# One hybrid encoder layer on one core: reciprocal square roots from eleven VectorE instructions to one GpSimd power, and an order chosen out of 24 drawn plans

## The chip, the core and the metric

The kernel runs on one core of a Trainium2 chip. The metric is the device time of one launch in microseconds (us); lower is better. The kernel before takes 2738.26 us (median of three runs, 2738.12 to 2742.08).

## What is computed

One layer of a bidirectional encoder on a sequence of 2048 tokens of width 1024, all in float32. A normed input is projected once, and the columns go to three groups of heads: attention in a window of 128, a state-space model that runs forward and backward in chunks of 128, and cross attention to 256 memory tokens. The three outputs are joined, projected and added to the input, and a squared-ReLU MLP follows.

```python
h = rmsnorm(x, norm_mix_w[i])
q, k, v, z, xbc, dt_raw, qx = jnp.split(h @ w_in[i], split_idx, axis=-1)
q = partial_rope(rmsnorm(q, q_norm_w[i]), pos)      # per head; k likewise
attn_out = windowed_gqa(q, k, v, attn_sink[i])
ssd_out = bidirectional_ssd(z, xbc, dt_raw, ...)    # ends in rmsnorm per group
xatt_out = memory_cross_attention(qx, mem, ...)     # rmsnorm of q, k and mem
x = x + jnp.concatenate([attn_out, ssd_out, xatt_out], axis=-1) @ w_out[i]
x = x + jnp.square(jax.nn.relu(rmsnorm(x, norm_mlp_w[i]) @ w_mlp_up[i])) @ w_mlp_down[i]
```

Every `rmsnorm` needs the reciprocal square root of a mean of squares: one number per token, or per token and head.

## The kernel before, in words

Matrix products in float32 precision are made of three faster ones: each operand is split into a high part (a cast on ScalarE) and a low part (a subtraction on VectorE or GpSimd), and high·high, high·low and low·high are added in PSUM. Most of TensorE's instructions are such products of a 128x128 stationary tile with 512 moving columns.

The program has three stages. **Stage 1** (`stage1`, L1113) goes over the sequence in two halves, the second half first. For each half it splits x, makes keys, values and time steps (`kv_products`, `kvdt_tiles`), sums the squares of the rows of x (`x_square`, `x_stats`), makes twelve columns of the convolved state-space input (`xbc_col`), and then queries for the memory and the window two token tiles at a time (`xattn_pair`, `q_pair`). In between run the memory's keys and the backward states. **Stage 2** goes over 16 token tiles with window attention and the forward state-space scan. **Stage 3** is the output projection of pairs of token tiles (`out_pair`), the norm before the MLP (`mid`), and the MLP (`seven` products in place of eight per 2x2 block).

The reciprocal square root is the function `rsqrt` (L497). It works on a small tile of 128 partitions by n numbers, where n is 2 to 16, and issues eleven VectorE instructions: two `tensor_scalar` (a first guess from the bits of the number, and minus half the number), and three Newton steps of three instructions. Each reads what the one before wrote. It is called 40 times: 24 times in stage 1 (keys 4, memory 2, rows of x 2, memory queries 8, window queries 8) and 16 times in stage 3 (8 in `out_pair`, 8 in `mid`). In `head_norm` (L666) the result is multiplied by the row's factor on VectorE, then by the whole tile on GpSimd; `rope` (L691) rotates the first 16 columns of each head with four GpSimd instructions per tile, and only then TensorE transposes the tile.

No engine's order is written by hand. Each call such as `nc.vector.tensor_tensor` is recorded as an operation with a cost and its dependencies (`Program.add`, L201; costs in `cost`, L176). `plan` (L287) then plays the program through with these costs: of the operations of an engine that are ready it takes the one that stands first in the program among those that are "safe", which means that a margin has passed since their last input was ready. `margin` (L275) sets that margin by the kinds of the two operations: 3000 ns where a DMA waits, 5000 ns before a product that fills half the array, 1500 ns after a DMA, 400 ns where TensorE waits for another engine, 800 ns otherwise. The plan also hands out the eight PSUM banks, and never lets GpSimd and a VectorE instruction on SBUF run at once. `schedule` issues all operations in that order, so in the profile they all bear the line L414.

Names in the views: `small` holds the small tiles of the norms, `const` and `late` hold tables; X, W, A, B, C, E and Z are regions of SBUF that are used anew in each stage; `bank` is PSUM.

Of the kernel before, what the change touches and what calls it, by code (L numbers as in the profile page):

```python
# [10 lines left out]
F32 = mybir.dt.float32  # L11
F32R = mybir.dt.float32r
I32 = mybir.dt.int32
AF = mybir.ActivationFunctionType
ALU = mybir.AluOpType
# [4 lines left out]
P = 128  # L20
# [15 lines left out]
NCOL, NROW = sum(n for _, n in COLS), sum(n for _, n in ROWS)  # L36
# [37 lines left out]
class Program:  # L74
# [101 lines left out]
    def cost(self, eng, name, args, kw, aps):  # L176

        n = max(self.free(args[0] if args else kw["out"]), 1)
        isap = lambda x: isinstance(x, (View, bass.AP))
        if eng == "PE":  # L180
            if name == "transpose":
                return 109
            return 108 if n < 32 else n / 2.4 + 13 if args[1].dtype == F32R and n >= 256 else n * 4 / 2.4 + 6
        if eng == "ACT":
            n_ap = sum(isap(kw.get(k)) for k in ("bias", "scale", "accum_out"))
            return 93 * n_ap + 0.834 * n + (50 if isinstance(args[1], View) and args[1].psum else 93)
        if eng == "DVE":
            if name == "reciprocal":
                return 69 + 6.25 * n
            n = max([n] + [self.free(a) for a in aps])  # L190
            if name == "memset":
                return 9 + 1.04 * n
            ap_scalar = any(isap(x) and self.free(x) == 1 for x in args[2:4]) and "scalar" in name
            fast = name in ("tensor_copy", "tensor_scalar") and not any(isinstance(a, View) and a.psum for a in aps)
            return 69 + (0.52 if fast else 1.041) * n + (61 if ap_scalar else 0)
        if eng == "POOL":
            bcast = any(d[0] == 0 and d[1] > 1 for a in aps[1:] for d in a.ap.ap[1:])
            return 148 + (1.667 if bcast else 2.1) * n if name == "tensor_tensor" else 40 + 1.6 * n
        return 475

# [70 lines left out]
            self.vuse[v] += 1  # L271
        ops.append(o)

    @staticmethod
    def margin(o, q):  # L275

        if q.eng == "SP":
            return 3000
        if q.eng == "PE" and q.half:
            return 5000  # L280
        if o.eng == "SP":
            return 1500
        if q.eng == "PE" and o.eng != "PE":
            return 400
        return 0 if o.eng == q.eng or o.eng == "PE" else 800

    def plan(self):  # L287

        engs = ["", "PE", "ACT", "POOL", "DVE", "SP"]
        free = dict.fromkeys(engs, 0.0)  # L290
# [5 lines left out]
        bank, vend = {}, {}  # L296
# [3 lines left out]
        order = []  # L300
# [5 lines left out]
        while len(order) < len(ops):  # L306
            best = None
            for e in engs:
                t = free[e]
# [14 lines left out]
            o = ops[i]  # L324
            if e == "PE" and pe_half and i != pe_last + 1 and pe_last + 1 in re:
# [4 lines left out]
                o = ops[i]  # L330
            elif e == "PE" and pe_mode and not o.half:
                same = [q for q in re if ops[q].half]
                if same:
# [4 lines left out]
                    o = ops[i]  # L338
# [9 lines left out]
            if o.new:  # L348
                got = [heapq.heappop(banks) for _ in o.new]
# [8 lines left out]
            d = o.dur  # L358
            if e == "PE":
                if o.half and pe_half == (o.dur, not o.half[1]):  # L360
                    d, pe_half = 20, None
# [32 lines left out]
                if q.ndep == 0:  # L394
                    heapq.heappush(future[q.eng], (q.ready, q.idx))
        order.sort()
        self.span, self.order, self.bank = max(free.values()), order, bank

    def schedule(self):
        self.plan()  # L400
# [60 lines left out]
class Hybrid:  # L461
# [34 lines left out]

    def rsqrt(self, pool, v, n):  # L497

        nc = self.nc
        y = pool.tile([P, 32], F32, "nr_y")[:, :n]  # L500
        h = pool.tile([P, 32], F32, "nr_h")[:, :n]
        t = pool.tile([P, 32], F32, "nr_t")[:, :n]
        nc.vector.tensor_scalar(y.bitcast(I32), v.bitcast(I32), -0.5, 1597463007.0, ALU.mult, ALU.add)
        nc.vector.tensor_scalar(h, v, -0.5, None, ALU.mult)
        for _ in range(3):
            nc.vector.tensor_tensor(t, y, y, ALU.mult)
            nc.vector.tensor_tensor(t, t, h, ALU.mult)
            nc.vector.scalar_tensor_tensor(y, t, 1.5, y, ALU.add, ALU.mult)
        return y

    def ps(self):
# [2 lines left out]

    def constants(self):
        nc, a = self.nc, self.a
        sizes = dict(ident=128, ones=128, eps=1, cols=NCOL, r1=16)
        self.mem.use("const", F32, **{"c_" + k: (n, 1) for k, n in sizes.items()})
        sizes = dict(triU=128, triL=128, amask=768, rows=NROW, dt=512, acs=512, wst=512, dec=512, edge=48, negA=32, nsk=8)
        self.mem.use("late", F32, **{"c_" + k: (n, 1) for k, n in sizes.items()})  # L520

        def c(name, shape):
            return self.mem.tile([P] + shape, F32, "c_" + name)

        self.eps = c("eps", [1])
        nc.vector.memset(self.eps, EPS)
        nc.scalar.activation(self.eps, self.eps, AF.Copy)
        self.ident = c("ident", [P])
        make_identity(nc, self.ident)
        self.ones = c("ones", [P])  # L530
        nc.gpsimd.memset(self.ones, 1.0)
        self.triU = c("triU", [P])
        self.triL = c("triL", [P])
        for t, sgn in ((self.triU, 1), (self.triL, -1)):
            nc.gpsimd.affine_select(out=t, in_=self.ones, compare_op=ALU.is_ge, fill=0.0, base=0,
                                    pattern=[[sgn, P]], channel_multiplier=-sgn)
        self.mask = c("amask", [6 * P])
        nc.gpsimd.memset(self.mask, 0.0)
        for o, sgn in ((0, 1), (2, -1), (3, 1), (5, 1)):
            m = self.mask[:, o * P:(o + 1) * P]  # L540
            nc.gpsimd.affine_select(out=m, in_=m, compare_op=ALU.is_ge, fill=NEG, base=0,
                                    pattern=[[sgn, P]], channel_multiplier=-sgn)

        cols, rows = c("cols", [NCOL]), c("rows", [NROW])
        first = NCOL - 256
        self.load(cols[:, :first], a["cols"][:, :first])

        def cut(t, table, name, shape=None):
            at = sum(n for k, n in table[:[k for k, _ in table].index(name)])
            v = t[:, at:at + dict(table)[name]]  # L550
            return v.rearrange("p (a b) -> p a b", a=shape[0]) if shape else v

        self.w_mix, self.w_mem, self.w_mlp, self.w_ssd, self.cb, self.sd = (
            cut(cols, COLS, n) for n in ("w_mix", "w_mem", "w_mlp", "w_ssd", "cb", "sd"))
        self.cw, self.cos, self.sin = cut(cols, COLS, "cw", (NXC,)), cut(cols, COLS, "cos", (NJ,)), cut(cols, COLS, "sin", (NJ,))
        for v in (cut(cols, COLS, "cw"), self.cb):
            nc.vector.tensor_scalar(v, v, 0.5, None, ALU.mult)
        self.qw, self.kw, self.xqw, self.xkw, self.sink, self.dtb, self.al = (
            cut(rows, ROWS, n) for n in ("qw", "kw", "xqw", "xkw", "sink", "dtb", "al"))
        self.r1 = c("r1", [NJ])  # L560
        self.dt = c("dt", [NJ, 32])
        self.acs = c("acs", [NJ, 32])
        self.wst = c("wst", [NJ, 32])
        self.dec = c("dec", [NJ, 32])
        self.edge = c("edge", [NXC, 4])
        self.negA = c("negA", [32])
        self.nsk = c("nsk", [8])
        yield
        self.load(cols[:, first:], a["cols"][:, first:])
        self.load(rows, a["rows"].rearrange("(o n) -> o n", o=1).broadcast_to([P, NROW]))  # L570
        nc.vector.tensor_scalar(self.qw, self.qw, 0.125, None, ALU.mult)
        nc.vector.tensor_tensor(self.xkw, self.xkw, self.xqw, ALU.mult)
        nc.scalar.activation(self.negA, self.al, AF.Exp)
        nc.vector.tensor_scalar(self.negA, self.negA, -1.0, None, ALU.mult)
        nc.vector.tensor_scalar(self.nsk, self.sink, -1.0, None, ALU.mult)
        yield

    def memory(self):
        m = self.mem
        m.use("small", F32, nr_y=(32, 3), nr_h=(32, 3), nr_t=(32, 3), nr_v=(32, 3), xmx=(32, 2), xsm=(32, 2),  # L580
              amx=(32, 3), ang=(32, 3), asm=(32, 3), aes=(32, 3), rm=(32, 1), s2=(32, 2))

    def memory1(self):
# [1181 lines left out]
```

## Time and profile before

| | us |
|---|---|
| runs: median (lowest, highest) | 2738.26 (2738.12, 2742.08) |
| profiled execution: span, first to last instruction | 2734.9 |
| what lies around the span, median less span | 3.4 |
| TensorE products busy | 2706.3 (99%) |
| VectorE busy | 1900.8 (70%) |
| ScalarE busy | 1331.6 (49%) |
| GpSimd busy | 554.2 (20%) |

A busy TensorE is not TensorE at its peak, since the ends of its instructions are modelled; but where it is not busy it waits. In a row of waits, "PE bank <- POOL B" reads: TensorE, about to write PSUM, was released last by a GpSimd instruction that wrote region B. In a timeline a row gives start, length, engine, output and inputs, the count of merged instructions, and in brackets the idle time ahead of it and who ended it.

### The profile page before, as it was taken

Reading aid. Unit: us, or ns where it says so; the run is one execution under the profiler, and the core shown is the slowest. Engines: PE = TensorE matmul, PEld = TensorE weight load, DVE = VectorE, ACT = ScalarE, POOL = GpSimd, SP = SyncE. Lnnn points to the kernel's source line nnn. Section 1 sums busy time; section 2 is a strip of 40 time slices with the busy share of each in tenths; the row PEclk is TensorE's granted clock in tenths of the full one; section 3 lists DMA queues with packets and bytes.
Section 4 is the critical chain, followed back from the end, with each engine's and each line's share of the span. In section 5 each row is a group of like instructions: output and inputs, shape, how many; then the busy total and the mean of one; then the engine's idle time right before and its main releaser. Section 6 shows DMA issues by size and latency. Waiting matters only on the chain.

```text
span 2734.9 us, 37074 instructions
## 1 busy us (share of the span) xinstructions
PE 2706.3 (99%) x13486; PEld 2236.3 (82%) x13486; DVE 1900.8 (70%) x3102; ACT 1331.6 (49%) x2229; POOL 554.2 (20%) x488
## 2 busy tenths in 40 slices
PE   8999999999999999999999999999999999999999
PEld 7788887787778888788888888888888888888887
DVE  6884689956677686776666785857757584857666
ACT  6545534353567676733333543535353443535352
POOL 3203444455445554410101000000000000000000
PEclk9999999999999999999999999999999999999999
DMA  6651446545877786865555954536272745435241
GB/s 239 213 182 59 133 147 190 172 158 177 268 251 235 214 257 205 271 204 200 193 192 202 342 195 146 170 102 214 80 259 93 253 162 169 154 119 197 90 165 62
DMA packets 264886, 501.40 MB, mean 183 GB/s; under 512 B 26096, under 2 KB 99072, under 8 KB 264704
## 3 DMA queue, kind: packets, MB, share of 16 engines
q1 hardware_dynamic: 264704, 499.04, 55.3%
q8 instruction: 106, 1.74, 0.3%
q14 instruction: 76, 0.62, 0.1%
HBM read 381.51 MB, written 117.45 MB: 182 GB/s over the span
## 4 chain that ended last, share of the span: by engine, by line
PE 92%; DVE 2%; POOL 2%; ACT 1%; issue 1%; DMA 1%; SPq 0%; DVEq 0%; ACTq 0%; POOLq 0%
PE bank L414 92%; POOL B L414 1%; DVE B L414 1%; DVE A L414 1%; POOL E L414 1%; DVE small L414 0%; DMA Z<-in_w_out_dram 0%; ACT C L414 0%; SPq L414 0%; DMA W<-erow_d 0%; DVE W L414 0%; ACT A L414 0%; ACT B L414 0%; POOL W L414 0%; DVE X L414 0%
## 5 line engine op out<-in xcount | busy, mean ns | idle before, releaser
L414 PE MATMUL bank<-X,late 128*128 128x512 f32 x1792 | 552.3, 389 | 0.0
L414 PE MATMUL bank<-A,E 128*128 128x512 f32 (+2 forms) x1152 | 404.8, 380 | 1.1 <-ACT A L414 0.7
L414 PE MATMUL bank<-X,A 128*128 128x512 f32 (+1 forms) x1264 | 396.1, 390 | 0.2 <-DMA A<-v_d 0.2
L414 PEld LDWEIGHTS bank<-X,late 128*128 128x128 f32 x1792 | 336.3, 188 | 69.6
L414 PE MATMUL bank<-late,C 128*128 128x512 f32 x896 | 348.6, 389 | 0.0
L414 PE MATMUL bank<-late,E 128*128 128x512 f32 x896 | 348.6, 389 | 0.0
L414 PE MATMUL bank<-W,X 128*128 128x512 f32 (+1 forms) x1536 | 339.4, 373 | 6.5 <-ACT W L414 5.8
L414 PE MATMUL bank<-X,W 128*128 128x512 f32 x1344 | 324.3, 398 | 0.7 <-ACT E L414 0.6
L414 PE MATMUL bank<-X,X 128*128 128x512 f32 x1216 | 317.6, 401 | 0.6 <-DVE X L414 0.6
L414 PEld LDWEIGHTS bank<-W,X 128*128 128x128 f32 x1536 | 265.8, 190 | 51.5 <-ACT W L414 5.8
L414 PEld LDWEIGHTS bank<-X,W 128*128 128x128 f32 x1344 | 250.8, 189 | 55.8 <-issue 3.4
L414 PEld LDWEIGHTS bank<-X,X 128*128 128x128 f32 x1216 | 225.2, 188 | 56.0 <-issue 8.9
L414 PEld LDWEIGHTS bank<-A,E 128*128 128x128 f32 x1152 | 211.7, 188 | 43.0 <-issue 2.8
L414 PEld LDWEIGHTS bank<-X,A 128*128 128x128 f32 (+1 forms) x1264 | 192.5, 173 | 50.5 <-issue 3.5
L414 DVE TENSOR_TENSOR A<-Z,late 128x1024 fp32r<-128x1024 f32 x100 | 121.9, 1221 | 149.0 <-ACT late L414 142.6
L414 DVE TENSOR_TENSOR B<-B,bank 128x512 f32<-128x512 f32 x286 | 189.7, 680 | 33.3 <-PE bank L414 32.6
L414 PEld LDWEIGHTS bank<-late,E 128*128 128x128 f32 x896 | 168.2, 188 | 34.9
L414 PEld LDWEIGHTS bank<-late,C 128*128 128x128 f32 x896 | 168.2, 188 | 34.8
L414 ACT CAST late<-Z 128x1024 fp32r<-128x1024 f32 x100 | 105.1, 1051 | 140.0 <-PE bank L414 101.3
L414 ACT ACTIVATE C<-C,small 128x384 f32<-128x384 f32 (+1 forms) x256 | 143.8, 598 | 36.0 <-DVE small L414 35.9
L414 ACT ACTIVATE W<-W 128x512 f32<-128x512 f32 x224 | 134.4, 627 | 48.9 <-DVE W L414 45.9
L414 DVE SCALAR_TENSOR_TENSOR B<-B,const 128x1022 f32<-128x1022 f32 (+1 forms) x96 | 146.0, 1524 | 3.9 <-ACT B L414 3.0
(178 smaller groups left out, 4259.3 us busy)
## 6 DMA issues: line engine op xcount, KB each, us to landing
X<-xc_d SPq DMA_DIRECT2D x112, 1024.0 KB
xc_d<-E SPq DMA_DIRECT2D x56, 512.0 KB
Z<-in_w_z_dram SPq DMA_DIRECT2D x32, 512.0 KB
W<-erow_d SPq DMA_DIRECT2D x64, 256.0 KB
X<-in_w_up_dram SPq DMA_DIRECT2D x32, 512.0 KB
A<-in_w_up_dram SPq DMA_DIRECT2D x32, 512.0 KB
X<-in_w_down_dram SPq DMA_DIRECT2D x32, 512.0 KB
A<-in_w_down_dram SPq DMA_DIRECT2D x32, 512.0 KB
```

Source lines behind the costliest of these rows:

```text
L414: o.fn(*[fix(x) for x in o.args], **{k: fix(x) for k, x in o.kw.items()})
```

## The change

First, `rsqrt` becomes one GpSimd instruction, `tensor_tensor` with the operation power, whose second operand is a constant tile `root` that holds -0.5. The tiles `nr_h` and `nr_t` go. Second, the planner charges such a power 500 + 40 n ns. Third, `plan` calls the old planning loop (now `draw`) 24 times. The first draw has the old margins; in each of the others every one of the five margins is multiplied by a random factor between 0.5 and 1.6. The order with the shortest modelled span is kept. In this program it is draw 18 (counted from 0), with margins of 1707, 7040, 1021, 365 and 679 ns in place of 3000, 5000, 1500, 400 and 800.

```diff
@@ cost @@
         if eng == "POOL":
             bcast = any(d[0] == 0 and d[1] > 1 for a in aps[1:] for d in a.ap.ap[1:])
+            if ALU.pow in args:
+                return 500 + 40 * n
@@ margin, plan @@
-    @staticmethod
-    def margin(o, q):
+    MARGIN = (3000, 5000, 1500, 400, 800)
+    PLANS = 24
+
+    def margin(self, o, q):
 
+        m = self.margins
         if q.eng == "SP":
-            return 3000
+            return m[0]
         if q.eng == "PE" and q.half:
-            return 5000
+            return m[1]
         if o.eng == "SP":
-            return 1500
+            return m[2]
         if q.eng == "PE" and o.eng != "PE":
-            return 400
-        return 0 if o.eng == q.eng or o.eng == "PE" else 800
+            return m[3]
+        return 0 if o.eng == q.eng or o.eng == "PE" else m[4]
 
     def plan(self):
+        rng = np.random.default_rng(1)
+        kept = None
+        ndep = [o.ndep for o in self.ops]
+        for n in range(self.PLANS):
+            for o, d in zip(self.ops, ndep):
+                o.ndep, o.ready, o.safe, o.end = d, 0.0, 0.0, -1.0
+            self.margins = [m * f for m, f in zip(self.MARGIN, rng.uniform(0.5, 1.6, 5) if n else np.ones(5))]
+            got = self.draw()
+            if kept is None or got[0] < kept[0]:
+                kept = got
+        self.span, self.order, self.bank = kept
+
+    def draw(self):
...
-        self.span, self.order, self.bank = max(free.values()), order, bank
+        return max(free.values()), order, bank
@@ rsqrt @@
-        nc = self.nc
         y = pool.tile([P, 32], F32, "nr_y")[:, :n]
-        h = pool.tile([P, 32], F32, "nr_h")[:, :n]
-        t = pool.tile([P, 32], F32, "nr_t")[:, :n]
-        nc.vector.tensor_scalar(y.bitcast(I32), v.bitcast(I32), -0.5, 1597463007.0, ALU.mult, ALU.add)
-        nc.vector.tensor_scalar(h, v, -0.5, None, ALU.mult)
-        for _ in range(3):
-            nc.vector.tensor_tensor(t, y, y, ALU.mult)
-            nc.vector.tensor_tensor(t, t, h, ALU.mult)
-            nc.vector.scalar_tensor_tensor(y, t, 1.5, y, ALU.add, ALU.mult)
+        self.nc.gpsimd.tensor_tensor(y, v, self.root[:, :n], ALU.pow)
         return y
@@ constants @@
+        self.root = c("root", [32])
+        nc.gpsimd.memset(self.root, -0.5)
```

The products and their number are the same; their order on every engine is planned anew. Three places show how.

VectorE at the first norm of keys (the second half of the sequence, its first four token tiles), before: the last five instructions of the reciprocal square root (`small`, 128x8), between the time steps' softplus in B (128x256) and products of a convolution column (128x512).

```order
L414 TENSOR_TENSOR small_87<-small_87 128x8
L414 TENSOR_SCALAR B_101<-B_101 128x256
L414 TENSOR_TENSOR small_87<-small_87 128x8
L414 RECIPROCAL B_101<-B_101 128x256
L414 TENSOR_TENSOR B_101<-bank_77,Z_102 128x512
L414 TENSOR_TENSOR B_101<-bank_80,Z_102 128x512
L414 TENSOR_TENSOR B_101<-bank_78,Z_102 128x512
L414 SCALAR_TENSOR_TENSOR small_87<-small_87 128x8
L414 COPY late_89<-B_101 128x4
L414 MEMSET B_101 128x2
L414 TENSOR_TENSOR B_101<-B_101 128x256
L414 TENSOR_TENSOR small_87<-small_87,const_88 128x8
```

The same place after, from the sum of squares on:

```order
L433 TENSOR_REDUCE small_87<-B_101 128x8
L433 TENSOR_SCALAR small_87<-small_87 128x8
L433 TENSOR_TENSOR late_89<-E_103,late_89 128x32 x4
L433 TENSOR_TENSOR small_87<-small_87,const_88 128x8
L433 TENSOR_SCALAR B_101<-B_101 128x256
L433 RECIPROCAL B_101<-B_101 128x256
```

The multiplication by the row's factor (`small<-small,const`) moved ahead of the softplus and of the convolution, which stood between it and the sum of squares.

GpSimd at the same place, before: four low parts of weights (128x1024), then the multiplication of the keys by the result (128x512) and the rotations.

```order
L414 TENSOR_TENSOR W_0_98<-Z_102,W_0_97 128x1024 x4
L414 TENSOR_TENSOR B_101<-B_101,small_87 128x512
L414 TENSOR_TENSOR E_103<-B_101,const_88 128x32 x2
L414 TENSOR_TENSOR B_101<-E_103 128x2x8
L414 TENSOR_TENSOR E_103<-B_101,const_88 128x32
```

GpSimd after; the two rows that write `small` are the powers for the rows of x and for these keys:

```order
L433 TENSOR_TENSOR W_0_98<-Z_102,W_0_97 128x1024
L433 TENSOR_TENSOR small_87<-const_88 128x8
L433 TENSOR_TENSOR W_0_98<-Z_102,W_0_97 128x1024 x2
L433 TENSOR_TENSOR small_87<-small_87,const_88 128x8
L433 TENSOR_TENSOR B_101<-B_101,small_87 128x512
L433 TENSOR_TENSOR E_103<-B_101,const_88 128x32 x3
```

The power of the keys now stands on GpSimd's queue behind the third of the four low parts of weights; the fourth moved behind the rotations. On TensorE the first transposition of these keys has 103 products of 512 columns ahead of it before, and 72 after.

TensorE at the last pair of window queries, near the end of stage 1, before: the transpositions of the queries (`bank<-const,B`) stand inside a column of z (24 products into bank_83, from X and W), after 19 of its products.

```order
L414 MATMUL bank_83<-X_0_95,W_0_98 128x512
L414 MATMUL bank_83<-X_0_95,W_0_97 128x512
L414 MATMUL bank_78<-const_88,B_101 128x128 x4
L414 MATMUL bank_83<-X_0_96,W_0_97 128x512
L414 MATMUL bank_83<-X_0_95,W_0_98 128x512
```

After, the same transpositions in the same column of z, which now is in bank_84:

```order
L433 MATMUL bank_80<-X_0_95,W_0_98 128x512
L433 MATMUL bank_84<-X_0_93,W_0_97 128x512
L433 MATMUL bank_84<-X_0_94,W_0_97 128x512
L433 MATMUL bank_84<-X_0_93,W_0_98 128x512
L433 MATMUL bank_82<-const_88,B_101 128x128 x4
L433 MATMUL bank_84<-X_0_93,W_0_97 128x512
```

They moved from behind the nineteenth product of the column to behind the third.

More of the change, by code (lines that the diff above doesn't have):

```diff
@@ L516, in constants @@
         nc, a = self.nc, self.a
-        sizes = dict(ident=128, ones=128, eps=1, cols=NCOL, r1=16)
+        sizes = dict(ident=128, ones=128, eps=1, root=32, cols=NCOL, r1=16)
         self.mem.use("const", F32, **{"c_" + k: (n, 1) for k, n in sizes.items()})
@@ L579, in memory @@
         m = self.mem
-        m.use("small", F32, nr_y=(32, 3), nr_h=(32, 3), nr_t=(32, 3), nr_v=(32, 3), xmx=(32, 2), xsm=(32, 2),
+        m.use("small", F32, nr_y=(32, 3), nr_v=(32, 3), xmx=(32, 2), xsm=(32, 2),
               amx=(32, 3), ang=(32, 3), asm=(32, 3), aes=(32, 3), rm=(32, 1), s2=(32, 2))
```

## The prediction

> **What bounds the kernel now.** I read the page first, for the share of each engine, then TensorE's stretches, to see where it is not busy, and then who ended its waits.
>
> ```profile
> span 2734.9 us, 37074 instructions
> ...
> PE 2706.3 (99%) x13486; PEld 2236.3 (82%) x13486; DVE 1900.8 (70%) x3102; ACT 1331.6 (49%) x2229; POOL 554.2 (20%) x488
> ```
>
> TensorE (PE) is the bound: it works 2706.3 of 2734.9 us, so all waiting together is 28.6 us, and the number of its products does not change. What the edit can give is a part of these 28.6 us, and of what a lowered clock costs. The stretches of TensorE (start and end, length, busy time and products, granted clock, DMA share, GB/s) show where that is:
>
> ```profile
> 0.00:120.00 120.00, 108.19 (x549) 0.97 0.67 224
> 120.00:680.00 560.00, 554.74 (x2886) 1.00 0.48 154
> 680.00:1175.00 495.00, 487.07 (x3102) 0.99 0.78 243
> 1175.00:2735.00 1560.00, 1556.33 (x6954) 1.00 0.50 172
> ```
>
> 11.8 us of waiting lie in the first 120 us, 5.3 in the rest of stage 1, 7.9 in stage 2, and 3.7 in stage 3 and its start. The chain of waits has stage 3 as one piece:
>
> ```profile
> 1174.13 1557.22 PE bank L414 x6957
> ```
>
> So the sixteen reciprocal square roots after 1174 us are hidden behind products, and removing VectorE's part of them gives nothing. The same row prices a product: 1557.22 / 6957 = 0.224 us. Who ended TensorE's waits (us in all, times, longest):
>
> ```profile
> PE bank L414 <- POOL B L414: 8.1, 7, 3.3
> PE bank L414 <- ACT W L414: 5.8, 1, 5.8
> ```
>
> The 5.8 us are the wait for the first data at the start, which the change does not touch. The 8.1 us are waits for the rotated heads that GpSimd writes into B, at the end of a chain with the reciprocal square root in it. They are the largest thing that the change can reach.
>
> **The change part by part.** *The root itself.* First what eleven small instructions take at the first norm of keys. VectorE there:
>
> ```profile
> 47.68 0.67 DVE L414 TENSOR_REDUCE small<-B 128x8 f32<-128x512 f32 x1
> 48.39 2.65 DVE L414 TENSOR_SCALAR small<-small 128x8 f32<-128x8 f32 x3
> ...
> 56.26 0.15 DVE L414 SCALAR_TENSOR_TENSOR small<-small 128x8 f32<-128x8 f32 x1
> ```
>
> GpSimd:
>
> ```profile
> 48.55 2.39 POOL L414 TENSOR_TENSOR W<-Z,W 128x1024 fp32r<-128x1024 f32 x1 [1.15 <-ACT W L414]
> ...
> 56.99 1.07 POOL L414 TENSOR_TENSOR B<-B,small 128x512 f32<-128x512 f32 x1 [1.07 <-DVE small L414]
> ...
> 59.73 1.21 POOL L414 TENSOR_TENSOR B<-E 128x16 f32<-128x16 f32 x1
> ...
> 61.11 0.21 POOL L414 TENSOR_TENSOR B<-E 128x16 f32<-128x16 f32 x1
> ```
>
> TensorE:
>
> ```profile
> 61.38 0.33 PE L414 MATMUL bank<-const,B 128*128 128x128 f32 x1 [3.35 <-POOL B L414]
> ```
>
> Behind the sum of squares (`TENSOR_REDUCE`) the root runs from about 48.6 to 56.4, 7.8 us, since the time steps' and the convolution's instructions stand between its steps, and since three VectorE instructions on eight numbers took 2.65 us while GpSimd's 2.39 us instruction ran beside them. The opposite is there too: the same small GpSimd step takes 0.21 us free and 1.21 us at 59.73.
>
> The trace has no power. Its nearest rows, by tile and by group (min/median/max or mean, ns), are
>
> ```profile
> L414 POOL TENSOR_TENSOR B<-E x64: 213/318/1384, 59.7 to 681.4; 128x16 f32<-128x16 f32 x32, 128x64 f32<-128x64 f32 x32
> L414 POOL TENSOR_TENSOR W<-Z,W 128x1024 fp32r<-128x1024 f32 x38 | 96.0, 2530 | 204.1 <-ACT W L414 201.9 <-PE bank L414 2.2
> L414 DVE TENSOR_TENSOR small<-small x273: 97/164/2390, 37.5 to 1521.3; 128x8 f32<-128x8 f32 x46, 128x4 f32<-128x4 f32 x40, 128x2 f32<-128x2 f32 x27, 128x16 f32<-128x16 f32 x24
> ```
>
> A GpSimd instruction on a small tile takes 0.32 us; the lower bound of a power is that. The upper is 2.53 us, the longest common one, on 64 times the numbers of the largest root. A power is several operations per number, but there are at most 16 numbers per partition: I take 0.8 us, near the lower row. Undisturbed, eleven instructions at 0.164 us are 1.8 us, so even alone the power is 1.0 us shorter, and where other work stands between the steps it saves several. On VectorE 40 roots of 11 x 0.164 = 72 us of work go; since VectorE is busy 70% and TensorE 99%, that is worth nothing by itself. GpSimd gains 40 x 0.8 = 32 us on 554 (20%), hidden likewise, except where the power stands in its queue ahead of something awaited.
>
> The Trainium skill, "GPSIMD Engine Reference", section 4.1, speaks against the move: elementwise work belongs on VectorE, GpSimd being about twice as slow for two inputs. The trace agrees on the small steps (0.318 against 0.164 us), but the rule compares one instruction with one; by its factor a root would be 0.33 us, and by the sum it is 0.8, so either way it is shorter than eleven.
>
> *First keys.* By the order shown above, the power runs behind the third low part of weights, which in the trace is the one that ends at 48.55 + 2.39 = 50.94. With the power (0.8), the row's factor (about 0.2) and a free GpSimd, the multiplication starts at about 52.5 in place of 56.99, so the keys are ready some 4.5 us earlier. But TensorE comes earlier too: 72 products stand ahead of its transposition in place of 103, and 31 x 0.224 = 6.9 us. The wait would be 3.35 - 4.5 + 6.9 = 5.8, that is +2.4. At the other end it goes altogether, -3.35, if the rotations, no longer held by the convolution as at 59.73, are quicker by as much. I take +1.0, nearer the first end, which is worked out from the order.
>
> *Second keys.* Their sum of squares, GpSimd's multiplication and TensorE's wait:
>
> ```profile
> 74.78 0.68 DVE L414 TENSOR_REDUCE small<-B 128x8 f32<-128x512 f32 x1
> ```
>
> ```profile
> 89.59 1.04 POOL L414 TENSOR_TENSOR B<-B,small 128x512 f32<-128x512 f32 x1 [12.21 <-DVE small L414]
> ```
>
> ```profile
> 94.71 0.33 PE L414 MATMUL bank<-const,B 128*128 128x128 f32 x1 [2.13 <-POOL B L414]
> ```
>
> GpSimd sat idle for 12.21 us until the root was through. In the new order this transposition has 146 products of 512 columns ahead of it in place of 219, so TensorE comes 73 x 0.224 = 16.4 us earlier. VectorE is quicker still: between the two sums of squares the order has 22 instructions in place of 48, and between the second sum and the row's factor 10 in place of 30. At the old pace (48 in 74.78 - 47.68 = 27.1 us, 30 in 89.59 - 74.78 = 14.8 us) that is 14.7 and 9.9 us less, 24.6 in all. The 2.13 us go, with 8 us to spare. The clock goes with it; the stretches around the waits (granted clock behind the busy time):
>
> ```profile
> 58.00:66.00 8.00, 4.65 (x15) 0.79 0.06 24
> 90.00:100.00 10.00, 7.87 (x32) 0.83 0.66 205
> 354.00:362.00 8.00, 6.53 (x37) 1.00 0.31 114
> ```
>
> Behind the 3.35 us wait 8 x (1 - 0.79) = 1.7 us of clock are lost, behind the 2.13 us wait 10 x (1 - 0.83) = 1.7, and behind several waits under 1 us (354 to 362) none. So the second keys give -2.1 - 1.7 = -3.8, from 0 (VectorE's instructions wait for other things, and the room is used up) to -3.8; the first keys keep their 1.7.
>
> The Trainium skill, "TensorE: Matmul & The Clock Gate", Part 1, has the clock halved after at least one idle window of about 3.4 us. Here 2.13 us sufficed, so the measurement decides; by the rule taken strictly this term would be -2.1, and the sum 1.7 us less of a gain.
>
> *The other five waits* for B are 8.1 - 3.35 - 2.13 = 2.6 us, at query pairs. The last of them:
>
> ```profile
> 674.55 2.82 POOL L414 TENSOR_TENSOR B<-B,small 128x1024 f32<-128x1024 f32 x1 [6.64 <-DVE small L414]
> ```
>
> ```profile
> 681.22 0.66 PE L414 MATMUL bank<-const,B 128*128 128x128 f32 x4 [0.31 <-POOL B L414]
> ```
>
> GpSimd waits 6.64 us for the norm's result; the transpositions move up by 16 products, 16 x 0.224 = 3.6 us. With the idle time gone that leaves 3 us of room, and the wait of 0.31 goes. For all five -2.6, from -2.6 to +2.6 where the moved transpositions meet the same lateness.
>
> *Factors of the rows of x*, second half. VectorE's root and TensorE behind it:
>
> ```profile
> 350.58 1.56 DVE L414 TENSOR_SCALAR small<-const 128x8 int32<-128x8 int32 x2
> ...
> 355.02 0.17 DVE L414 COPY const<-small 128x8 f32<-128x8 f32 x1
> ```
>
> ```profile
> 357.87 0.27 PE L414 MATMUL bank<-const 128*8 128x128 f32 x1 [0.32 <-DVE A L414]
> 358.76 2.46 PE L414 MATMUL bank<-X,W 128*128 128x512 f32 x8 [0.62 <-ACT E L414]
> ```
>
> The root took 4.4 us; a power takes 0.8, and the two waits behind it, 0.94, go: -0.9, from 0.
>
> *The rest of the plan.* Of 28.6 us there remain 28.6 - 8.1 - 5.8 - 0.9 = 13.8, which the chosen draw deals out anew by other margins. It was chosen among 24 for a short modelled span, but the waits that exist are what the model did not see. I take a tenth, -1.4; the ends are -5 and +5, about a third.
>
> The sum: +1.0 - 3.8 - 2.6 - 0.9 - 1.4 = -7.7. The profiled span would become 2734.9 - 7.7 = 2727.2; the 3.4 us between the span and the median of the runs stay, so the time is 2738.26 - 7.7 = **2730.6 us**. The 0.2% that a measurement can tell from no change are 5.5 us.
>
> **The rivals.** *The planner spends the room (0.22).* It puts the transpositions nearer to the shortened chains (6.9 and 3.6 us above), so the waits are as large as they were: their size is the planner's error, not the chain. Then only the rows' factors give, 2738.26 - 0.9 = **2737.4**. For it speaks the first keys' place, where the move up exceeds the shortening; against it the second keys and the last pair, where the chain shortens by more.
>
> *The power is slow (0.13).* At 2.53 us, by itself or because VectorE holds it as it held the step at 59.73 for 1.0 us more, each chain is 1.7 us later than planned with 0.8. TensorE waited at eight of the 24 chains of stage 1 (seven for B, one for the rows' factors); at these eight it shows, 8 x 1.7 = 13.6, and 13.6 - 7.7 = +5.9: **2744.2**, slower. It decides from 0.8 + 7.7 / 8 = 1.8 us per power on. For it: GpSimd is the slower engine on small tiles; against it: at most 16 numbers per partition.
>
> The Trainium skill, "SBUF — State Buffer", section "Who interferes with whom", has the port pair of VectorE and GpSimd as an exclusive lock held for a whole instruction. The 2.65 us and the 1.21 us rows above agree.
>
> *Smaller margins lay transfers bare (0.10).* The kept draw lets a product follow a modelled landing by 1021 ns in place of 1500, and a DMA its input by 1707 in place of 3000. Transfers already stand in the chain of waits:
>
> ```profile
> 714.52 8.66 DMA W<-erow_d
> ```
>
> If the lateness of stage 2 doubles, 7.9 us of waiting and 495 x 0.01 = 5.0 us of clock are added: 12.9 - 7.7 = +5.2, **2743.5**. Against it: an issue allowed earlier lands earlier as well.
>
> **How the numbers follow.** The forecast has 0.55. Its ends are -7.7 - (1.0 + 3.35 + 1.7) - 3.6, where the first wait goes with its clock and the rest comes out at its lower end, about -17, and about -4, where the other five waits come back and a part of the second: of it 0.43 is faster by over 5.5 us, 0.12 within. The first rival (0.22) is within, but for 0.02 faster. The slow power gives 0.09 slower and 0.04 within, the transfers 0.05 and 0.05; 0.03 slower is taken from the forecast's share within for a plan that comes out badly elsewhere. Together: faster 0.45, same 0.38, slower 0.17. The range reaches from 2720, the forecast's lower end, to 2746, a little above the slow power, which leaves out under 2 in 10.
>
> **What would show it.** The rows of GpSimd that write `small`: about 0.8 us each, and not above 1.8. TensorE's waits for B: 3 to 5 us in place of 8.1, nearly all of it at the first keys, none at the second; a clock of 1.00 at the second keys' transposition, so that the first 120 us are at 0.98 or above; the small VectorE instructions without 2.4 us maxima. Stage 2 should keep its 7.9 us, stage 3 its one piece. The forecast is wrong if the sum of waits for B stays near 8 us, spread over new places (the first rival), if the powers take 2 us (the second), or if the stretch from 680 to 1175 has over 12 us of idle time (the third).

## The result and the profile after

The changed kernel takes 2748.91 us (median of five runs, 2746.38 to 2752.01), the kernel before 2738.26 beside it: 10.65 us more, a ratio of 1.0034 with a 95% interval of 1.0021 to 1.0047. Slower, where 2730.6 was forecast and the range ended at 2746.

The profiled execution has a span of 2746.4 us. TensorE's stretches (start and end, length, busy time and products, granted clock, DMA share, GB/s):

```profile
0.00:120.00 120.00, 108.13 (x559) 0.99 0.71 240
120.00:680.00 560.00, 549.82 (x2853) 1.00 0.47 149
680.00:1175.00 495.00, 482.82 (x3069) 0.99 0.78 240
1175.00:2746.00 1571.00, 1567.84 (x7009) 1.00 0.51 172
```

The idle time is 11.9, 10.2, 12.2 and 3.2 us, where it was 11.8, 5.3, 7.9 and 3.7. So the loss shows in the rest of stage 1, where the queries are normed (+4.9), and in stage 2 (+4.3). Who ended TensorE's waits:

```profile
PE bank L433 <- POOL B L433: 15.4, 11, 4.3
PE bank L433 <- ACT W L433: 6.7, 1, 6.7
```

The waits for GpSimd's rotated heads, the ones that the change was to shorten, have nearly doubled, from 8.1 us at 7 places to 15.4 at 11. GpSimd's powers in order of time, one of each width (start, length, in brackets the idle time ahead and its releaser):

```profile
51.00 1.64 POOL L433 TENSOR_TENSOR small<-small,const 128x8 f32<-128x8 f32 x1
...
302.48 2.90 POOL L433 TENSOR_TENSOR small<-small,const 128x16 f32<-128x16 f32 x1 [7.32 <-DVE small L433]
...
1202.79 0.71 POOL L433 TENSOR_TENSOR small<-small,const 128x2 f32<-128x2 f32 x1 [6.29 <-DVE small L433]
...
1221.96 1.02 POOL L433 TENSOR_TENSOR small<-small,const 128x4 f32<-128x4 f32 x1 [1.48 <-DVE small L433]
```

The four lengths lie on one line, 0.40 us + 0.156 us per number in a partition. The planner charges 0.50 + 0.04 n: 0.82 us in place of 1.64 at eight numbers, and 1.14 in place of 2.90 at sixteen. TensorE's order is made for roots that are over by then. VectorE too has a wait that it did not have:

```profile
DVE small L433 <- POOL small L433: 26.2, 12, 3.5
```

VectorE stands in front of the multiplication by the row's factor until the power is through, with whatever is queued behind.

### The profile page after: what moved, and what is told of

The parts are those of the page before. It is cut to its first block, busy times and chain, and to the rows that moved or that the text cites. A ratio compares the mean times of both kernels' runs of the same rounds, so it can differ in the third digit from the quotient of the medians.

```text
span 2746.4 us, 36640 instructions
## 1 busy us (share of the span) xinstructions
PE 2708.6 (99%) x13486; PEld 2240.1 (82%) x13486; DVE 1853.0 (67%) x2662; ACT 1332.7 (49%) x2229; POOL 615.7 (22%) x529
## 4 chain that ended last, share of the span: by engine, by line
PE 90%; DVE 3%; POOL 3%; DMA 2%; ACT 1%; issue 1%; SPq 0%; DVEq 0%; POOLq 0%; ACTq 0%
PE bank L433 90%; POOL B L433 1%; DVE B L433 1%; POOL E L433 1%; DVE A L433 1%; POOL small L433 1%; DVE small L433 1%; DVE X L433 1%; DMA W<-erow_d 1%; DMA Z<-in_w_z_dram 0%; DMA Z<-in_xT_dram 0%; DMA B<-xbc_d 0%; ACT C L433 0%; ACT B L433 0%; DMA B<-mix_d 0%
```

## The experiments

In each the difference is taken to the kernel before on the same chip, beside it. "Idle" is TensorE's. "Waits for B" are TensorE's waits for region B, the rotated heads; theories A to D are those of the expectations. Where powers are executed as multiplications by -0.5, GpSimd's instruction, its queue place and its dependences stay, and only its length falls, to 0.22 us on sixteen numbers where nothing holds it.

### The drawn order, with the power's length changed

First the length alone, in the changed kernel's own order.

```diff
@@ schedule @@
                 o = ops[i]
+                if ALU.pow in o.args:
+                    o.args = (*o.args[:3], ALU.mult)
                 o.fn(*[fix(x) for x in o.args], **{k: fix(x) for k, x in o.kw.items()})
```

> The order of every engine is that of the changed kernel, instruction for instruction; only the 40 powers are executed as GpSimd multiplications by -0.5, so that the reciprocal square roots are left out. Theory A (slow power: the planner takes a power for 0.82 to 1.14 us in stage 1, it takes 1.64 to 2.9, and TensorE comes too early for the chains): TensorE's waits for GpSimd's B fall from 15.4 to 6 us or less, and the time from 2748.9 to 2735-2740. Theory B (smaller margins: the waits come from the drawn margins, whatever a power takes): waits in stage 2 stay and the time stays at 2745 or above.

Measured: 2736.18 us, 3.5 below the kernel before (2739.65; ratio 0.9987, 0.9978 to 0.9996). TensorE's waits for B and its stretches:

```profile
PE bank L435 <- POOL B L435: 5.8, 5, 3.0
```

```profile
120.00:680.00 560.00, 556.84 (x2902) 1.00 0.49 154
680.00:1175.00 495.00, 482.13 (x3062) 0.99 0.78 239
```

Waits for B fall from 15.4 to 5.8 us, the queries' stretch from 10.2 us idle to 3.2. That is theory A. Stage 2 keeps 12.9 us, as theory B had it, but the time falls below the kernel before all the same.

```diff
@@ schedule @@
                 o = ops[i]
+                if ALU.pow in o.args:
+                    o.fn(*[fix(x) for x in o.args])
                 o.fn(*[fix(x) for x in o.args], **{k: fix(x) for k, x in o.kw.items()})
```

> The order of the changed kernel again; each power is issued twice, one after the other, into the same tile, so each chain is longer by 1.6 to 2.9 us in stage 1. Theory A: each of the eleven places where TensorE waits for B grows by about the length of its power, 11 x 2.1 = 23 us, and some places that now have room begin to wait: 2768-2785. Theory B: the powers have room, so 2748-2755.

Measured: 2799.75 us, +60.1 (ratio 1.0222, 1.0208 to 1.0236), above even A's range.

```profile
PE bank L435 <- POOL B L435: 41.4, 16, 6.0
```

Three points of one curve in one order: nearly no length -3.5, the power +10.65, twice the power +60.1. The first length costs 14 us, the second 49. The waits for B grow with it, from 5.8 us at 5 places to 15.4 at 11 and 41.4 at 16, which fits chains whose room the first length has used up. They are 26.0 us of the second step; TensorE's busy time grows by 12.4 us, at a lower granted clock (mean 0.993 in the profiled run in place of 0.996).

The wide powers alone made cheap:

```diff
@@ schedule @@
+                if ALU.pow in o.args and self.free(o.args[0]) == 16:
+                    o.args = (*o.args[:3], ALU.mult)
```

> The order of the changed kernel; only the eight powers of 16 numbers per partition are executed as multiplications by -0.5 (these roots are left out), the other 32 stay powers. If the wide ones carry nearly all of the loss, as in the old order (2752.2 with all, 2740.3 without the wide ones): 2737-2741. If the loss goes by the time that powers take in stage 1, of which the wide ones have about half: 2742-2744.

Measured: 2739.4 us, +0.3 (1.0002, 0.9993 to 1.0011). Waits for B:

```profile
PE bank L435 <- POOL B L435: 8.5, 6, 4.3
```

Eight powers of sixteen numbers carry 10.65 - 0.3 = 10.4 us of the loss; the other 32 together 0.3 + 3.5 = 3.8. Each of these differences is uncertain by 2.5 to 3.5 us either way. The first of the two expectations holds: the loss does not go by the time that powers take in all.

### The order of before, with powers

To take the planner out, GpSimd's power was put into the order of before, at the place of the first of the eleven instructions. The edits of the three runs after this one are shown against this one.

```diff
@@ rsqrt @@
+        nc.roots[first] = (y, v, nc.root[:, :n])
+        nc.gone.update(range(first + 1, first + 11))
@@ schedule @@
+                if i in self.gone:
+                    continue
...
+                if i in self.roots:
+                    gp.tensor_tensor(*[fix(x) for x in self.roots[i]], ALU.pow)
+                    continue
...
```

> The order of the kernel before on every engine, planned with the eleven VectorE instructions; at the place of the first of them GpSimd issues one power, and the other ten are left away. So nothing is planned anew: TensorE's order is that of before, row for row. A (what is bad is the power, 1.64 to 2.9 us on GpSimd and in VectorE's way): 2742-2750. C (what is bad is the new plan, which spends the shortened chains and moves other things; the power itself is shorter than the spread of eleven instructions, 4 to 10 us at most places): waits for B fall from 8.1 to 4 us or less and the time to 2729-2736.

Measured: 2752.23 us, +13.2 (1.0050, 1.0037 to 1.0062). So theory C, to which I had moved by then, falls: without any new plan the power costs more than in the drawn one. GpSimd at the first pair of window queries:

```profile
313.05 1.30 POOL L424 TENSOR_TENSOR E<-B,const 128x128 f32<-128x128 f32 x3
315.06 3.38 POOL L422 TENSOR_TENSOR small<-small,const 128x16 f32<-128x16 f32 x1 [0.71 <-DVE small L424]
318.41 0.31 POOL L424 TENSOR_TENSOR B<-E 128x64 f32<-128x64 f32 x1
```

TensorE there:

```profile
319.47 0.95 PE L424 MATMUL bank<-const,B 128*128 128x128 f32 x4 [2.62 <-POOL B L424]
```

The power at 315.06 is the next tile's root. It stands between two steps of this tile's rotation, and the transposition waits 2.62 us for the second. On VectorE the same root ran beside the rotation. It is not the root's own chain that is late, but the chain in whose queue it was put. TensorE waits behind such a power at four places, 2.62, 2.57, 1.35 and 2.54 us (at 319, 334, 361 and 680 us), 9.1 of the 17.4 us of waits for B.

```diff
@@ schedule @@
-                    gp.tensor_tensor(*[fix(x) for x in self.roots[i]], ALU.pow)
+                    gp.tensor_tensor(*[fix(x) for x in self.roots[i]], ALU.mult)
```

> The same with the powers executed as multiplications by -0.5 (the roots are left out). A: 10 us or more below its twin with powers, as with the drawn plan. C: within 3 us of its twin, since in the old order the chains have the room of eleven instructions; 2728-2735.

Measured: 2736.39 us, -2.7 (0.9990, 0.9981 to 0.9999): 15.9 below its twin with powers, so A and not C. Its stage 2:

```profile
680.00:1175.00 495.00, 483.89 (x3078) 0.99 0.78 241
```

11.1 us idle where the kernel before, in the same order of products, has 7.9. So that stretch varies by 3 us without any drawn margin, and the 12.2 us of the changed kernel are no sure sign of the margins.

```diff
@@ rsqrt @@
+        if n < 16:
             nc.roots[first] = (y, v, nc.root[:, :n])
             nc.gone.update(range(first + 1, first + 11))
```

> The order of the kernel before; the power only for roots of 2 to 8 numbers per partition (0.7 to 1.65 us), the eight roots of 16 numbers (2.9 us as a power) stay on VectorE. If the long powers cost anything in the old order, this is below the twin with all powers by 1 us or more; if not, the two agree within 2 us. C: 2730-2736.

Measured: 2740.25 us, +1.2 (1.0009, 1.0000 to 1.0018): 12.0 below the twin with all powers. Here too nearly all of it hangs on the eight wide roots, which in this run are exact and on VectorE.

```diff
@@ rsqrt @@
-        nc.roots[first] = (y, v, nc.root[:, :n])
-        nc.gone.update(range(first + 1, first + 11))
+        nc.roots[first + 10] = (y, v, nc.root[:, :n])
+        nc.gone.update(range(first, first + 10))
```

> The order of the kernel before once more, with the power at the place of the last of the eleven instructions in place of the first. GpSimd's queue then has it right ahead of the multiplication that uses it and never ahead of another tile's rotations, but each chain starts its root later. D (in the old order the power of 16 numbers costs by standing in GpSimd's queue ahead of rotations that TensorE waits for, as at 319 and 334 us): those two waits of 2.6 us go, 2743-2748. A (what counts is the length alone, 1.64 to 2.9 us at the end of each chain): every chain ends later than with the power at the first place, 2752-2765.

Measured: 2739.3 us, +0.2 (1.0000, 0.9991 to 1.0009), lower than even D expected. GpSimd at the same pair as above:

```profile
314.49 0.46 POOL L424 TENSOR_TENSOR E<-B,const 128x128 f32<-128x128 f32 x1
314.91 1.33 POOL L424 TENSOR_TENSOR B<-E 128x64 f32<-128x64 f32 x3
316.19 2.91 POOL L422 TENSOR_TENSOR small<-small,const 128x16 f32<-128x16 f32 x1
```

TensorE:

```profile
316.15 0.60 PE L424 MATMUL bank<-const,B 128*128 128x128 f32 x4
```

The same power, 2.91 us long, now starts behind the rotation; the transposition has no wait, and the 13 us are gone. Of the four waits one is left, of 0.44 us. In this order, then, nearly all of the loss was the place in GpSimd's queue, and most chains had room for the power at their end: waits for B are 8.5 us at 5 places, against 8.1 at 7 in the kernel before, with 3.8 us at the first keys and 1.8 at 667 us. Against the cheap powers, 2.7 us below the kernel before, 2.9 us are left to the length.

### The planner

```diff
@@ cost @@
-                return 500 + 40 * n
+                return 400 + 156 * n
```

> The changed kernel with the planner's price of a power set to what the trace shows, 400 + 156 n ns in place of 500 + 40 n; the 24 draws stay, so the order is planned anew. Theory A: waits for B fall to 8 us or less, 2734-2741. Theory B: still smaller margins of some kind, 2745-2750. A third reading, C (each new plan of this model lands some us up or down, whatever is in it), allows anything from 2732 to 2750 and then shows in waits at other places than the norms.

Measured: 2747.55 us, +7.9 (1.0031, 1.0019 to 1.0044). A's number failed. The waits for B and TensorE's longest:

```profile
PE bank L433 <- POOL B L433: 9.7, 2, 7.9
```

```profile
58.88 0.47 PE L433 MATMUL bank<-const,B 128*128 128x128 f32 x1 [7.94 <-POOL B L433]
```

The right price ended the waits at the queries but for one of 1.8 us (two places for B are left, of eleven), but another draw is now the shortest (23 in place of 18), and it brings TensorE to the first keys 7.94 us too early.

The drawn plans without the power:

```diff
@@ rsqrt @@
-        self.nc.gpsimd.tensor_tensor(y, v, self.root[:, :n], ALU.pow)
+        nc.vector.tensor_scalar(y.bitcast(I32), v.bitcast(I32), -0.5, 1597463007.0, ALU.mult, ALU.add)
+        nc.vector.tensor_scalar(h, v, -0.5, None, ALU.mult)
...
```

> The kernel before, with its eleven VectorE instructions per root, and the 24 drawn plans. Theory A: no power, no mispriced chain, so 2733-2741, about as before. Theory B: the drawn margins alone bring the loss, 2744-2750, with stage 2's idle time above 11 us. C: anything from 2732 to 2750.

Measured: 2743.15 us, +3.5 (1.0016, 1.0007 to 1.0025), between A and B. The stretch of stage 2 has 8.9 us idle, not 11. So a drawn plan without any power is some 3.5 us longer than the old one; its draw (number 2) is not the one that the changed kernel keeps.

The power without the draws, that is with the old margins and one plan:

```diff
-    PLANS = 24
+    PLANS = 1
```

> The changed kernel with one plan in place of 24, drawn with the old margins; power and its price of 500 + 40 n as in the change. A (a power takes longer than the planner thinks): the loss from it stays, so above the kernel before by 5 or more, 2744-2748, with waits for B of 12 us or more. B (the drawn margins bring a part, some 4 us, as the idle time of 11 to 13 us between 680 and 1175 us in both kernels with a drawn plan suggests): 2741-2745, and that stretch back at 8 us. C (luck of the plan): no relation.

Measured: 2783.96 us, +45.9 (1.0165, 1.0151 to 1.0179), far outside both ranges. Its twin with cheap powers (this edit and the one of the first experiment together):

> The order of the run with the old margins, with the powers executed as multiplications by -0.5 (the roots are left out). A: below its twin with powers by 10 to 13 us, as with the drawn margins (2748.9 against 2736.2): 2731-2735. B: 4 us below the cheap run with drawn margins, 2732. C: the difference between twins is anything, since another plan has other places with room.

Measured: 2767.34 us, +29.3 (1.0105, 1.0091 to 1.0119). The length of the power is 45.9 - 29.3 = 16.6 us of it, much as in the two other orders (14.1 and 15.9), as A's difference had it; A's range failed. The other 29.3 us come with no power to speak of. Who ended TensorE's waits there, and the longest:

```profile
PE bank L435 <- ACT X L435: 20.0, 12, 7.5
```

```profile
766.33 8.22 PE L435 MATMUL bank<-X,X 128*128 128x512 f32 x24 [7.47 <-ACT X L435]
```

ScalarE ahead of that:

```profile
763.53 2.13 ACT L435 ACTIVATE C<-C,small 128x384 f32<-128x384 f32 x4 [0.50 <-DVE small L435]
765.57 1.32 ACT L435 ACTIVATE X<-Z,const 128x512 fp32r<-128x512 f32 x2
```

TensorE wants a split of z that is queued on ScalarE behind a tile's softmax. That is stage 2, in which no root is computed: the stretch from 680 to 1205 us has 29.5 us idle, at a granted clock of 0.96, where the kernel before has 7.8 us idle from 680 to 1174, at 0.99. Another plan with the same margins comes out worse there by nearly all of the 29 us.

With the right price and the old margins (the edits of `cost` and of `PLANS` together):

> Old margins, one plan, and the power at its measured price of 400 + 156 n. A: the planner now leaves room, so 5 us or more below the same with the old price, 2735-2741. C: as with drawn margins, the right price moves the waits to another place and gives less than 3 us.

Measured: 2759.43 us, +21.4 (1.0076, 1.0063 to 1.0090): 24.5 below the old price, where the same correction gave about 3 with the draws. A's difference holds, its range does not: waits for B fall from 19.9 to 3.4 us, but those for ScalarE's X only from 19.3 to 12.8.

The eleven instructions of before with the five margins that the changed one keeps (the edit of the planner is shown against the changed kernel's):

```diff
-    MARGIN = (3000, 5000, 1500, 400, 800)
-    PLANS = 24
+    MARGIN = (1707, 7040, 1021, 365, 679)
+    PLANS = 1
```

> The kernel before, eleven VectorE instructions per root, with one plan, drawn with the five margins that the changed kernel keeps (1707, 7040, 1021, 365, 679). B: the margins by themselves cost 3 to 6 us, 2742-2746, with 11 us or more of idle time between 680 and 1175 us. A alone: no difference from the kernel before, within 2 us. C: anything within 6 us either way.

Measured: 2744.96 us, +6.9 (1.0023, 1.0014 to 1.0033). Theory B's number holds, A's does not. But B's place fails: 680 to 1175 us has 10.2 us idle, and 9.5 us of its waits are one wait at the first keys (at 62.63 us).

A version made from this, short powers alone, rightly priced, and drawn:

```diff
@@ cost @@
+                return 400 + 156 * n
@@ rsqrt @@
+        if n < 16:
+            self.nc.gpsimd.tensor_tensor(y, v, self.root[:, :n], ALU.pow)
+            return y
...
```

> A version to beat both: the power only where it takes 1.65 us or less (2 to 8 numbers per partition), priced 400 + 156 n, eleven VectorE instructions for the eight roots of 16 numbers, 24 drawn plans. A (length of the power): no long power, right price, 2733-2740. C (each new plan lands up or down by itself): 2735-2755, with waits at places that have nothing to do with the roots.

Measured: 2742.43 us, +3.3 (1.0012, 1.0003 to 1.0021). It beats the changed kernel, not the one before, and A's range failed. Its waits for B are 4.9 us, fewer than the 8.1 before; what it loses stands elsewhere, as C had it. With all powers nearly free the order of before gained 2.7 us and the drawn one 3.5, so there is little to be had from shorter roots in them.

## Why the prediction was wrong

The step that failed is the price of the power: "I take 0.8 us, near the lower row". It takes 1.64 us on eight numbers and 2.90 on sixteen. The nearest rows, 0.32 and 2.53 us, were of instructions with another operation, chosen by how many numbers they handle; the same sixteen numbers take 0.22 us as a multiplication. The upper bound itself was too low for the wide ones. The Trainium skill, "GPSIMD Engine Reference", section 4.1, gives elementwise work to VectorE. The prediction set that aside by comparing one instruction with one; on sixteen numbers the one power takes 2.90 us, eleven VectorE instructions at 0.164 us take 1.8, so here the traces agree with the rule; on eight the power's 1.64 us are a little shorter than the eleven.

With the length taken away, in the same order, the kernel is 3.5 us faster than before; with it, 10.65 slower. The runs with cheap powers compute other numbers, but in the old order two runs with exact roots (short powers alone, and the late place) are also 12 to 13 us below the run with all powers. And 3.5 is not 7.7: with a power far shorter than 0.8 us the sum still fails by 4 us, so the power's price was not the only wrong term.

By the terms of the sum:

- **First keys: right, in part by luck.** +1.0 on 3.35 makes 4.35 us; the trace of after has 4.26 here (TensorE's first transposition of keys), and a clock of 0.91 over the 18 us around it, 18 x 0.09 = 1.6 us against 1.7. TensorE came 58.03 - 51.07 = 6.96 us earlier, as reckoned (6.9). The keys came 6.05 us earlier, not 4.5: the rotations took 2.0 us less than before, which made up for the longer power. The +1.0 was chosen between two ends, not worked out:

```profile
55.33 0.33 PE L433 MATMUL bank<-const,B 128*128 128x128 f32 x1 [4.26 <-POOL B L433]
```

- **Second keys: right.** Their transposition has no wait, and the stretch around it a full clock:

```profile
74.64 0.93 PE L433 MATMUL bank<-const,B 128*128 128x128 f32 x7
```

```profile
48.00:66.00 18.00, 13.50 (x53) 0.91 0.55 165
66.00:90.00 24.00, 24.00 (x115) 1.00 0.60 191
```

- **The other five waits: this is where the loss lies.** -2.6 was taken, with +2.6 as the far end. The other waits for B are 15.4 - 4.3 = 11.1 us now in place of 2.6, +8.5; 9.5 of them are at query pairs. The largest, at the third from last wide power, on GpSimd and on TensorE:

```profile
639.44 2.91 POOL L433 TENSOR_TENSOR small<-small,const 128x16 f32<-128x16 f32 x1 [1.63 <-DVE small L433]
642.32 1.91 POOL L433 TENSOR_TENSOR C<-C,late 128x1024 f32<-128x1024 f32 x1
644.34 1.91 POOL L433 TENSOR_TENSOR B<-B,small 128x1024 f32<-128x1024 f32 x1
```

```profile
648.60 0.66 PE L433 MATMUL bank<-const,B 128*128 128x128 f32 x4 [2.54 <-POOL B L433]
```

  Between that power and the multiplication that uses it stands another GpSimd instruction of 1.91 us. The working set the transpositions' 3.6 us of approach against GpSimd's idle time, and forgot that the power now takes its 2.9 us of that idle time. In the drawn order none of the eight wide powers stands ahead of another tile's rotation, and TensorE is timed for 1.14 us; that this mistiming and not the queue is what costs there is argued from the rows, since only the length was varied in that order. In the old order the queue place was varied, and it was nearly all of the loss. The prediction had named that place ("except where the power stands in its queue ahead of something awaited") and put nothing down for it. Even with cheap powers, in the drawn order, the waits at other places than the first keys are 5.8 - 3.0 = 2.8 us, no less than the 2.6 before: the -2.6 would not have come with a short power either.
- **Rows' factors: right in kind.** TensorE has no wait behind them any more; 1.45 us stand at the first transposition of keys just after.
- **The rest of the plan: wrong in sign.** All idle time grew by 37.8 - 28.6 = 9.2 us, and waits for B by 7.3, so the rest grew by 1.9 in place of falling by 1.4. TensorE's busy time grew by 2.3, which the sum did not have.

Of the rivals, the slow power had the mechanism, the sign and nearly the size: its cost of 13.6 us stands against 14.1 measured between the kernel and its cheap twin. That the sizes meet is partly luck: it reckoned eight places with one length, and there were eleven, with two lengths, and 9.6 of the 14.1 us are waits for B. It came out at 2744.2 because 7.7 us of gain were set against it; the runs show 3.5. Its break-even, 1.8 us, falls between the two widths, and the 32 powers below it cost 3.8 us, the eight above it 10.4. The planner that spends the room had a part in the drawn order, where TensorE was brought nearer for a root of 1.14 us; no run gives its size, and the old order, planned without any power, loses as much to the same length. The transfers were not: stage 2's 12.2 us passed the mark of 12 that I had set for them, but 11.1 came in the old order too, with the old margins.

What stays open is why the same planner lands anywhere from -3.5 to +29 us with powers that cost nearly nothing. The trace shows where (ScalarE's queue in stage 2, the first keys), but no experiment isolated what in the plan decides it. The planner's own model foresees much of the largest difference: at the change's price, `plan` reaches a modelled span of 2722.3 us with the old margins and 2697.1 with the draw that it keeps, 25 of the 35 us measured between those two kernels. Small differences it does not order: with eleven instructions per root the draw that it keeps is 1.7 us shorter by its model than the order of before (2697.8 against 2699.5), and 3.5 us longer as measured. No plan tried with a drawn or changed set of margins beat the kernel before with exact roots.

## What to carry to other kernels

An instruction that does the work of eleven need not be shorter than they are: before it replaces a chain, look for its own row, and where there is none, let the range reach past the longest row of its engine. When work moves to another engine, ask whose results are produced there: eleven steps on VectorE held up none of GpSimd's rotations here, one step in front of a rotation cost TensorE 2.6 us, and behind that rotation the same instruction cost it no wait. And a planner's new price and its new plan are two changes: run the new instruction in the old order, and the new order with the instruction made cheap, before either is blamed.

## What the runs showed of the hardware

A GpSimd power on 128 partitions took 0.71, 1.02, 1.64 and 2.90 us on 2, 4, 8 and 16 numbers per partition, against 0.22 us for a multiplication of the same sixteen. Where a VectorE instruction with all its tensors in SBUF (`X<-B,const,X`, `X<-Z,const,X`) had some 0.6 us left to run as it began, the power on sixteen took 3.35 to 3.38 us and the multiplication 0.65 to 0.67, some 0.45 us more in both. Where the VectorE instruction read PSUM (`C<-C,bank`, with 0.5 to 0.6 us left), they took 2.91 and 0.22 us, no longer than alone.
